# All tokens loaded channels first in the head of a fused hybrid block, two blocks un-normed in u's product

## The chip, the cores and the metric

The kernel runs on one NeuronCore of one Trainium2 chip. A core has a matrix engine (TensorE, PE in the profile), VectorE (DVE), ScalarE (ACT), GpSimd (POOL) and SyncE (SP, which here only issues DMAs), each with its own instruction queue, and 16 DMA engines that all queues share. The metric is the device time of one execution in microseconds. The kernel before takes 1488.93 us (median of three runs, 1485.58 to 1492.47).

## The reference

One layer of a hybrid block on 1040 tokens (16 learned meta tokens, then 1024), D = 1024, everything in float32:

```python
def _mixer(xn, w_in, ...):
    q, k, v, f_logit, u, gates = split(xn @ w_in)
    y_a = forgetting_attention(q, k, v, f_logit, b_forget) @ w_attn_out
    z = gelu(s5(u, ...))                       # 32 groups of 16 channels, 64 complex states each
    zg = z @ w_glu
    y_s = zg[:, :D] * sigmoid(zg[:, D:])
    g = sigmoid(gates)
    return (g[:, :D] * y_a + g[:, D:] * y_s) @ w_o

h = concatenate([meta, x])
h = h + mixer(rmsnorm(h, norm_mix_g))          # rmsnorm(x) = x * rsqrt(mean(x*x) + eps) * g
h = h + conv_ffn(rmsnorm(h, norm_ffn_g))
return rmsnorm(h, norm_final_g)[16:]
```

Only the first lines matter here: the norm of all tokens, u = xn @ w_u (512 columns), and what runs beside and behind it, which is the S5 recurrence on u and the gates' product.

## The kernel before, in words

Matrices are multiplied channels first: a product needs its input as "features", 128 channels on the partitions (8 chunks k) and tokens along the row. For float32 accuracy each operand is split into a high part (rounded to TensorE's fast format) and a low part, and each product takes three matmuls: high by high, low by high, high by low. `xhi` and `xlo` hold the normed features of all 1040 tokens and stay for the whole mixer. The low part on VectorE is called a cut here.

The head computes u in four token blocks, `UBLK` = 272, 256, 256 and 256 tokens, each in four column groups m. One block is 4 x 8 x 3 = 96 matmuls (`part`, L327 to L329). Rows of x come in nine `TILES` (16 meta tokens, then eight of 128).

- Block 0 is loaded channels first (`x0t` into `xa`). Its features are x times gamma only (L350 and L353); the norm's factor per token is applied to the finished product when VectorE copies it from PSUM (L377), from `rsB`, the factor spread to all partitions by three small transposes (L370) and a copy (L372).
- The other tiles are loaded with tokens on the partitions (`xt`). For each, ScalarE squares and sums (L174), VectorE and GpSimd make the factor (L176, L178), VectorE multiplies the tile by factor and gamma (L340), TensorE transposes it in eight pieces (L191), ScalarE makes the high parts (L193) and VectorE the low ones (L129). Tiles 0 to 2, which are block 0, go through the same at the end of u, since the later products need normed features.
- u is copied into `usb` (L387) and stored to `u_d` by 32 DMAs (L394); SyncE issues those of m = 0 and 2, GpSimd those of m = 1 and 3.
- The gates' product is called dense (L159 to L161), 72 matmuls a chunk of 128 columns. A chunk's weights are loaded by GpSimd (`raw`, L140), cast to the high part (L146), negated into `wlo` (L135) and completed there by an accumulating DMA of the same weights (L136). The weights of chunk 8, `g0`, have buffers of their own and an early load (L398).
- The S5 part (`ssm`) first makes tables of its discretised coefficients on VectorE (L1453 to L1459 and others). The scheduler may not start them ahead of the features of tiles 3 and 4 (`ready`). Then come four quarters q of the channels: load U from `u_d`, products, a scan on VectorE (L1748), output products (L1770, L1772), a store to `y_d`. The steps of the four quarters are woven into the dense chunks.
- Behind the dense chunks stand the forget gate (L518) and the GLU on z (L219), for which 32 SyncE DMAs load z from `y_d` (L543).

Which instruction comes when on each engine is not written out: a scheduler in the framework orders each engine's queue from the dependences, the buffers (a tag with so many of them) and its own estimates. Buffers are shared by tag: `Wi`, `Gm`, `sy`, `Tm`, `tq` belong to the S5 part and serve the head before it.

Of the kernel before, what the change touches and what calls it, by code (L numbers as in the profile page):

```python
# [50 lines left out]
def block_kernel(ctx, tc, x, meta, g1, x0t, g1t, w_q, w_k, w_v, w_f, w_u, w_g, b_f, w_ao, lam_d, bw_d, cw_d,  # L51
# [76 lines left out]
    def split_lo(eng, out_, src, hi):  # L128
        return eng.tensor_tensor(out_, src, hi.bitcast(F), ALU.subtract)  # L129
# [40 lines left out]
    def norm_factor(pl, src, n, bufs=10, sq=None):  # L170
# [3 lines left out]
        S.activation(sq[:n], src, AF.Square, accum_out=ss[:n])  # L174
        va = pl.tile([P, 1], F, tag="vr", name="vr", bufs=3)
        V.tensor_scalar(va[:n], ss[:n], 1.0 / D, EPS, ALU.mult, ALU.add)  # L176
        rs = pl.tile([P, 1], F, tag="rs", name="rs", bufs=bufs)
        GP.tensor_tensor(rs[:n], va[:n], nhalf[:n], ALU.pow)  # L178
        return rs
# [107 lines left out]
    xa = [sp.tile([P, 4, UN], F, tag="tq", name="xa", bufs=3) for _ in range(2)]  # L287
    g1T = n1.tile([P, KD], F, name="g1T")
    S.dma_start(g1T, g1t)
    S.dma_start(xm, meta)  # L290
# [15 lines left out]

    place = dict(zip((3, 4, 1, 2, 5, 6), xts))
    place[0] = xm

    def load_x(i):  # L310
        load(place[i], x[P * (i - 1):P * i])

    for i in range(1, 7):
        load_x(i)
# [19 lines left out]
    def factors(i):  # L334
        n = TILES[i][1]
        return norm_factor(n1, place[i][:n], n)

    def features(i, rs, behind=None):
        t, n = TILES[i]
        xn = V.scalar_tensor_tensor(out=place[i][:n], in0=place[i][:n], scalar=rs[:n], in1=g1B[:n],  # L340
                                    op0=ALU.mult, op1=ALU.mult)
        if behind is not None:
            after(xn, behind)
        return to_feature(place[i], n, xhi, xlo, t)[-1]

    first = [mm_ps() for _ in range(4)]
    for j in range(4):
        for k in (2 * j, 2 * j + 1):
            src, hi = xa[j // 2][:, k % 4], xhi[:, k, :UN]
            cp_ = S.activation(hi, src, AF.Copy, scale=g1T[:, k:k + 1])  # L350
            if k == 1:
                after(g1_load, cp_)
            V.scalar_tensor_tensor(out=xlo[:, k, :UN], in0=src, scalar=g1T[:, k:k + 1], in1=hi.bitcast(F),  # L353
                                   op0=ALU.mult, op1=ALU.subtract)
        S.copy(uh[j], uraw[j])
        split_lo(V, ul[j], uraw[j], uh[j])
        for m in range(4):
            for k in (2 * j, 2 * j + 1):
                part(first[m], m, k, 0, UN)
    for i in (7, 8):  # L360
        place[i] = sp.tile([P, D], F, tag="Tm", name="xt", bufs=2)
        load_x(i)

    rs0 = [factors(i) for i in range(3)]
    tp = t_ps()
    for i, rs in enumerate(rs0):
        t, n = TILES[i]
        rb = sp.tile([P, P], F, tag="wi", name="rb", bufs=2)
        V.tensor_copy(rb[:n], rs[:n].broadcast_to([n, P]))
        PE.transpose(tp[:, t:t + n], rb[:n], ident[:n, :n])  # L370
    rsB = sp.tile([P, UN], F, tag="wr", name="rsB", bufs=2)
    S.copy(rsB, tp[:, :UN])  # L372
    for i in (3, 4):
        ready = features(i, factors(i))
    n_log = len(ssm_log)
    for m in range(4):
        V.tensor_tensor(us[m][:, :, :UN // CH], by_chunks(first[m][:, :UN]), by_chunks(rsB), ALU.mult)  # L377

    for b, (t, n) in enumerate(UBLK[1:]):
        if b:  # L380
            for i in (3 + 2 * b, 4 + 2 * b):
                last = features(i, factors(i))
# [1062 lines left out]
def ssm(tc, after, sp, s_ps, ident, u_d, y_d, lam_d, bw_d, cw_d, d_sk, l_dt):  # L1445
# [27 lines left out]
    S.dma_start(ldt, l_dt.partition_broadcast(P))  # L1473

    lam = sm([P, 2, G])
    S.dma_start(lam, lam_d)
# [308 lines left out]
def _laid_out(x, meta_tokens, norm_mix_g, w_in, b_forget, w_attn_out, ssm_lambda_re, ssm_lambda_im, ssm_b_re, ssm_b_im,  # L1785
# [17 lines left out]
    x0 = _np.concatenate([meta_tokens, x[0]])[:UN]  # L1803
# [3 lines left out]
    return dict(x=x[0], meta=meta_tokens, g1=norm_mix_g[0], x0t=by_rows(x0.T), g1t=norm_mix_g[0].reshape(KD, P).T, w_q=blocks(q), w_k=blocks(k), w_v=by_rows(v),  # L1807
# [29 lines left out]
```

## Time and profile before

| | us |
|---|---|
| median of three runs | 1488.93 |
| lowest and highest run | 1485.58 and 1492.47 |
| span of the profiled execution | 1485.7 |
| TensorE busy in it | 1440.4 |
| VectorE, ScalarE, GpSimd busy | 1071.4, 712.2, 742.1 |
| first matmul | 7.32 |
| first dense matmul | 73.53 |
| first GLU matmul in an unbroken run | 239.17 |

Rows of the trace give the start, the duration, the engine, the source line, the operation with output and input tiles, the shape, and in brackets how long the engine stood idle just before and what released it. A row with "x4" joins four like instructions. Starts of matmuls, not their durations, show the pace, since they overlap in the pipeline.

### The profile page before, as it was taken

Reading aid. Unit: us, or ns where it says so; the run is one execution under the profiler, and the core shown is the slowest. Engines: PE = TensorE matmul, PEld = TensorE weight load, DVE = VectorE, ACT = ScalarE, POOL = GpSimd, SP = SyncE. Lnnn points to the kernel's source line nnn. Section 1 sums busy time; section 2 is a strip of 40 time slices with the busy share of each in tenths; the row PEclk is TensorE's granted clock in tenths of the full one; section 3 lists DMA queues with packets and bytes.
Section 4 is the critical chain, followed back from the end, with each engine's and each line's share of the span. In section 5 each row is a group of like instructions: output and inputs, shape, how many; then the busy total and the mean of one; then the engine's idle time right before and its main releaser. Section 6 shows DMA issues by size and latency. Waiting matters only on the chain. (4 is left out here: it accounts for less than half of the span.)

```text
span 1485.7 us, 26584 instructions
## 1 busy us (share of the span) xinstructions
PE 1440.4 (97%) x9712; PEld 1358.8 (91%) x9712; DVE 1071.4 (72%) x2173; ACT 712.2 (48%) x1384; POOL 742.1 (50%) x850
## 2 busy tenths in 40 slices
PE   7999997999999999999999999999999999998997
PEld 7989996998899999999888999999999999777886
DVE  6879648881566676647468987888877776788785
ACT  6434675541555665543546534444444445543433
POOL 1311125752456465524863144455544426789766
PEclk9999999999999999999999999999999999999999
DMA  6366571551127342047885135676653215765513
GB/s 246 86 157 157 128 163 50 177 160 43 48 79 178 93 111 90 26 148 256 257 158 185 57 109 141 178 199 188 174 143 100 84 57 180 286 203 148 168 40 114
DMA packets 91032, 206.72 MB, mean 139 GB/s; under 512 B 14651, under 2 KB 25531, under 8 KB 90517
## 3 DMA queue, kind: packets, MB, share of 16 engines
q1 hardware_dynamic: 69380, 159.73, 32.9%
q0 software_dynamic: 15296, 34.63, 13.2%
q10 hardware_dynamic: 6224, 10.65, 1.9%
q8 instruction: 77, 1.26, 0.3%
q14 instruction: 55, 0.44, 0.1%
HBM read 165.90 MB, written 69.35 MB: 158 GB/s over the span
## 5 line engine op out<-in xcount | busy, mean ns | idle before, releaser
L159 PE MATMUL mm<-xhi,whi 128*128 128x342 f32 (+2 forms) x488 | 159.4, 327 | 1.0 <-DVE q L129 1.0
L161 PE MATMUL mm<-xhi,wlo 128*128 128x342 f32 (+2 forms) x488 | 158.3, 325 | 0.0
L160 PE MATMUL mm<-xlo,whi 128*128 128x342 f32 (+2 forms) x488 | 157.7, 324 | 0.0
L1079 POOL TENSOR_TENSOR ov<-ov,og 128x1024 f32<-128x1024 f32 x21 | 51.1, 2434 | 125.6 <-ACT og L1078 121.7
L129 DVE TENSOR_TENSOR sw<-sf,sw 128x512 fp32r<-128x512 f32 x72 | 66.6, 925 | 50.0 <-ACT sw L1070 49.8
L1070 ACT CAST sw<-sf 128x512 fp32r<-128x512 f32 x72 | 44.9, 624 | 106.2 <-POOL sf L1196 74.5
L159 PEld LDWEIGHTS mm<-xhi,whi 128*128 128x128 f32 x488 | 91.9, 188 | 2.1 <-PE sp L714 0.8
L161 PEld LDWEIGHTS mm<-xhi,wlo 128*128 128x128 f32 x488 | 91.8, 188 | 0.3
L160 PEld LDWEIGHTS mm<-xlo,whi 128*128 128x128 f32 x488 | 91.9, 188 | 0.2
L763 ACT CAST th<-tp 128x256 fp32r<-128x256 f32 (+3 forms) x120 | 56.2, 472 | 62.5 <-PE tp L756 30.1
L129 DVE TENSOR_TENSOR tl<-tp,th 128x256 fp32r<-128x256 f32 (+3 forms) x120 | 65.2, 547 | 25.1 <-ACT th L763 23.7
L1196 POOL TENSOR_TENSOR sf<-raw,sf 128x512 f32<-128x512 f32 x36 | 59.1, 1641 | 44.8 <-DVE sw L129 44.7
L1196 POOL TENSOR_TENSOR sf<-raw 128x512 f32<-128x512 f32 x36 | 48.0, 1332 | 66.9 <-DMA raw<-in_w_up_dram 35.9
L221 PE MATMUL mm<-xhi,sw 128*128 128x258 f32 (+1 forms) x288 | 81.0, 281 | 0.0
L219 PE MATMUL mm<-xhi,sw 128*128 128x258 f32 (+1 forms) x288 | 80.8, 281 | 0.0
L220 PE MATMUL mm<-xlo,sw 128*128 128x258 f32 (+1 forms) x288 | 80.7, 280 | 0.0
L728 POOL TENSOR_SCALAR pt<-pt,nm 128x144 f32<-128x144 f32 (+4 forms) x72 | 51.8, 731 | 48.5 <-DVE nm L727 47.5
L1248 DVE SCALAR_TENSOR_TENSOR ov<-hv,cwt,ov 128x1024 f32<-128x1024 f32 x36 | 72.5, 2014 | 0.1
L1070 ACT CAST sw<-raw 128x512 fp32r<-128x512 f32 x70 | 43.0, 621 | 53.3 <-PE sp L221 25.5
L726 ACT ACTIVATE pt<-pt,nm 128x144 f32<-128x144 f32 (+4 forms) x72 | 52.9, 735 | 26.1 <-DVE nm L725 25.7
L719 DVE CUSTOM_DVE_ANT_0 pt<-sp,fb 128x328 f32<-128x328 f32 (+8 forms) x112 | 46.4, 430 | 20.0 <-PE sp L714 11.1
L756 PE MATMUL tp<-ident,pt 128*128 128x128 f32 (+1 forms) x360 | 58.3, 270 | 0.1
(708 smaller groups left out, 5702.1 us busy)
## 6 DMA issues: line engine op xcount, KB each, us to landing
raw<-in_w_up_dram SPq DMA_DIRECT2D x44, 512.0 KB, 3.6
t_d<-in_w_dn_dram POOLq DMA_DIRECT2D x44, 256.0 KB, 7.0
ar<-a_d SPq DMA_DIRECT2D x44, 256.0 KB, 5.1
wr<-t_d SPq DMA_DIRECT2D x44, 256.0 KB, 2.8
a_d<-ov SPq DMA_DIRECT2D x21, 512.0 KB, 2.6
wr<-in_w_dn_dram SPq DMA_DIRECT2D x33, 256.0 KB, 3.8
t_d<-in_w_dn_dram SPq DMA_DIRECT2D x22, 256.0 KB, 4.2
t_d<-t_d SPq DMA_DIRECT2D x22, 256.0 KB, 4.7
```

The lines of the kernel that those rows point to most:

```text
L129: return eng.tensor_tensor(out_, src, hi.bitcast(F), ALU.subtract)
L159: yield PE.matmul(ps, whi[:, i, :], ahi[:, i], start=(i == 0), stop=False)
L160: yield PE.matmul(ps, whi[:, i, :], alo[:, i], start=False, stop=False)
L161: yield PE.matmul(ps, wlo[:, i, :], ahi[:, i], start=False, stop=(i == k - 1))
L219: PE.matmul(ps, a[0][:, i], bh, start=(i == 0 and not joins), stop=False, skip_group_check=True)
L220: PE.matmul(ps, a[0][:, i], bl, start=False, stop=False, skip_group_check=True)
L221: PE.matmul(ps, a[1][:, i], bh, start=False, stop=(i == kh - 1), skip_group_check=True)
L756: PE.transpose(tp[:kn, o:o + n], p_[:n, k0:k0 + kn], ident[:n, :n])
L763: S.copy(th[:kn, z:tw], tp[:kn, z:tw])
L1070: S.copy(hi, src)
L1196: sums.append(GP.tensor_tensor(f_, a, b, op))
L1248: V.scalar_tensor_tensor(out=o, in0=h_[:, j:SEQ + j], scalar=cwc(j, m), in1=o, op0=ALU.mult, op1=ALU.add)
```

## The change

- All tokens are also loaded channels first: block 0 from `x0t` as before, blocks 1 to 3 from a new input `xbt` (3.1 MB in all). The rows of x are still loaded, for the squares. The load of gamma spread over all partitions goes.
- Blocks 0 and 1 go un-normed into u's product. The product is copied to `usb` by ScalarE, and after all of u VectorE multiplies the first 528 columns of each `usb` by the factors in place.
- Blocks 2 and 3 are multiplied by the factors channels first (`normed_features`) before their products. Blocks 0 and 1 go through the same behind the products of block 2, and `ready` is now the last of these.
- x is no longer transposed; each tile's factor is spread and transposed (nine small transposes).
- The first loads are cut into one k, one k, and then two each; the loads follow in the order block 1, rows 5 to 8, block 2, block 3, rows 1 to 4.
- Block 1 lies in the buffers `Wi`, block 2 in `Tm`, block 3 in `Gm`.
- Three small loads move from ScalarE's queue to GpSimd's.

```diff
-    S.dma_start(xm, meta)
+    GP.dma_start(xm, meta)
...
-    for j in range(4):
-        load(xa[j // 2][:, 2 * (j % 2):2 * (j % 2) + 2], x0t[:, 2 * j:2 * j + 2])
-        load(uraw[j], w_u[:, 2 * j:2 * j + 2])
-    xts = [sp.tile([P, D], F, tag=tag, name="xt", bufs=n) for tag, n in (("Wi", 2), ("Gm", 2), ("sy", 3)) for _ in range(n)]
-    g1B = xts.pop(4)
-    g1_load = S.dma_start(g1B, g1.partition_broadcast(P))
...
+    FIRST = [(0, 1), (1, 1), (2, 2), (4, 2), (6, 2)]
+    for k, n in FIRST:
+        load(xT[0][k // 4][:, k % 4:k % 4 + n], x0t[:, k:k + n])
+        load(uraw[k // 2][:, k % 2:k % 2 + n], w_u[:, k:k + n])
+
+    def load_block(b, tag):
+        xT[b] = [sp.tile([P, 4, UBLK[b][1]], F, tag=tag, name="xT", bufs=2) for _ in range(2)]
+        for h_ in range(2):
+            load(xT[b][h_], xbt[b - 1, :, 4 * h_:4 * h_ + 4])
...
+    load_block(1, "Wi")
+    for i in range(5, 9):
         load_x(i)
...
+    def factors(b):
+        tp = t_ps()
+        t0, n_ = UBLK[b]
+        for i in TB[b]:
+            t, n = TILES[i]
+            rs = norm_factor(n1, place[i][:n], n, behind=head[0])
+            rb = rbs[:n, i % 3]
+            V.tensor_copy(rb, rs[:n].broadcast_to([n, P]))
+            PE.transpose(tp[:, t - t0:t - t0 + n], rb, ident[:n, :n])
+        S.copy(spread[b], tp[:, :n_])
+
+    def features(b, k):
+        t, n = UBLK[b]
+        src, hi = xT[b][k // 4][:, k % 4], xhi[:, k, t:t + n]
+        cp_ = S.activation(hi, src, AF.Copy, scale=g1T[:, k:k + 1])
+        cut = V.scalar_tensor_tensor(out=xlo[:, k, t:t + n], in0=src, scalar=g1T[:, k:k + 1], in1=hi.bitcast(F),
+                                     op0=ALU.mult, op1=ALU.subtract)
+        return cp_, cut
+
+    def normed_features(b):
+        t, n = UBLK[b]
+        for q in range(2):
+            V.tensor_tensor(xT[b][q], xT[b][q], spread[b].unsqueeze(1).broadcast_to([P, 4, n]), ALU.mult)
+        return [features(b, k)[1] for k in range(KD)][-1]
...
+    load_block(2, "Tm")
+    load_block(3, "Gm")
+    for i in range(1, 5):
         load_x(i)
...
     for m in range(4):
-        V.tensor_tensor(us[m][:, :, :UN // CH], by_chunks(first[m][:, :UN]), by_chunks(rsB), ALU.mult)
...
+        S.copy(us_part(0, m), by_chunks(first[m][:, :UN]))
+    for k in range(KD):
+        features(1, k)
+    for b in (2, 3):
+        factors(b)
+    for m in range(4):
+        ps = u_product(1, m)
+        S.copy(us_part(1, m), by_chunks(ps[:, :UBLK[1][1]]))
+    for b in (2, 3):
+        last = normed_features(b)
+        if b == 3:
+            for q in (0, 1):
+                factors(q)
+            n_log = len(ssm_log)
+            for q in (0, 1):
+                ready = normed_features(q)
         for m in range(4):
-            ps = mm_ps()
-            for k in range(KD):
-                part(ps, m, k, t, n)
-            S.copy(us[m][:, :, t // CH:(t + n) // CH], by_chunks(ps[:, :n]))
-        if b == 2:
-            for i in range(3):
-                features(i, rs0[i], last)
+            ps = u_product(b, m)
+            S.copy(us_part(b, m), by_chunks(ps[:, :UBLK[b][1]]))
+    for m in range(4):
+        ub = us[m][:, :, :rs01.shape[1] // CH]
+        V.tensor_tensor(ub, ub, by_chunks(rs01), ALU.mult)
...
-    S.dma_start(ldt, l_dt.partition_broadcast(P))
+    GP.dma_start(ldt, l_dt.partition_broadcast(P))
...
-    S.dma_start(lam, lam_d)
+    GP.dma_start(lam, lam_d)
```

More of the change, by code (lines that the diff above doesn't have):

```diff
@@ L168, in run, with norm_factor @@
             pass
-    def norm_factor(pl, src, n, bufs=10, sq=None):
+    def norm_factor(pl, src, n, bufs=10, sq=None, behind=None):
         if sq is None:
@@ L173, in norm_factor @@
         ss = pl.tile([P, 1], F, tag="ss", name="ss", bufs=3)
-        S.activation(sq[:n], src, AF.Square, accum_out=ss[:n])
+        sa = S.activation(sq[:n], src, AF.Square, accum_out=ss[:n])
+        if behind is not None:
+            after(sa, behind)
         va = pl.tile([P, 1], F, tag="vr", name="vr", bufs=3)
@@ L332, in by_chunks @@
         return a.rearrange("p (n j) -> p j n", j=CH)
[L334 to L344, printed above, removed]
-    first = [mm_ps() for _ in range(4)]
@@ L347, in block_kernel @@
[L347 to L356, printed above, removed]
+    head = []
@@ new lines, in block_kernel @@
+    TB = [(0, 1, 2), (3, 4), (5, 6), (7, 8)]
+    spread = {}
+    rbs = sp.tile([P, 3, P], F, tag="dt8", name="rb", bufs=1)
+    rs01 = sp.tile([P, UN + UBLK[1][1]], F, tag="wr", name="rsB", bufs=2)
+    spread[0], spread[1] = rs01[:, :UN], rs01[:, UN:]
+    for b in (2, 3):
+        spread[b] = sp.tile([P, UBLK[b][1]], F, tag="wi", name="rsB", bufs=2)
+    def factors(b):
[8 more added lines that the diff above has]
+        S.copy(spread[b], tp[:, :n_])
@@ new lines, in u_product, with us_part @@
+    def u_product(b, m):
+        ps = mm_ps()
+        for k in range(KD):
+            part(ps, m, k, *UBLK[b])
+        return ps
+    def us_part(b, m):
+        t, n = UBLK[b]
+        return us[m][:, :, t // CH:(t + n) // CH]
+    first = [mm_ps() for _ in range(4)]
+    for k0, n in FIRST:
+        j, sl = k0 // 2, slice(k0 % 2, k0 % 2 + n)
+        for k in range(k0, k0 + n):
+            features(0, k)
+        cp_ = S.copy(uh[j][:, sl], uraw[j][:, sl])
+        split_lo(V, ul[j][:, sl], uraw[j][:, sl], uh[j][:, sl])
@@ L357, in block_kernel @@
         for m in range(4):
-            for k in (2 * j, 2 * j + 1):
+            for k in range(k0, k0 + n):
                 part(first[m], m, k, 0, UN)
-    for i in (7, 8):
-        place[i] = sp.tile([P, D], F, tag="Tm", name="xt", bufs=2)
+    head.append(cp_)
+    load_block(2, "Tm")
+    load_block(3, "Gm")
+    for i in range(1, 5):
         load_x(i)
[L364 to L370, printed above, removed]
```

26 lines of the change are left out of this document (10 added, 16 removed).

## The prediction

> **What bounds the kernel now.** I read the page first, then the windows of the head, then the order in time on TensorE. The page says which engine sets the length.
>
> ```profile
> span 1485.7 us, 26584 instructions
> ...
> PE 1440.4 (97%) x9712; PEld 1358.8 (91%) x9712; DVE 1071.4 (72%) x2173; ACT 712.2 (48%) x1384; POOL 742.1 (50%) x850
> ```
>
> TensorE is idle for only 45 us in all (1485.7 - 1440.4). The windows (start and end, then busy time of each engine, granted clock, DMA share, GB/s) show where some of that idle time lies.
>
> ```profile
> 20.00:40.00 20.00, 16.87 (x119) 16.41 (x119) 18.31 (x57) 9.66 (x20) 3.96 (x6) 0.83 0.31 124
> ...
> 80.00:100.00 20.00, 17.28 (x110) 16.63 (x109) 12.43 (x31) 7.04 (x16) 1.74 (x5) 0.91 0.78 184
> 100.00:120.00 20.00, 20.00 (x137) 19.75 (x135) 19.75 (x33) 8.70 (x18) 1.58 (x3) 1.00 0.54 112
> ```
>
> Two stretches matter: the head up to 100 us, which the change rewrites, and the one before the GLU, shown further down. From 100 us on TensorE is busy throughout. TensorE in time:
>
> ```profile
> 7.32 0.60 PE L327 MATMUL mm<-xhi,uh 128*128 128x272 f32 x1 [7.32 <-ACT uh L355]
> ...
> 22.05 0.60 PE L191 MATMUL sp<-ident,xt 128*128 128x128 f32 x4
> 22.48 0.60 PE L191 MATMUL tp<-ident,xt 128*128 128x128 f32 x4
> ...
> 26.21 1.12 PE L191 MATMUL sp<-ident,xt 128*128 128x128 f32 x4 [3.13 <-DVE vr L176]
> 31.59 0.41 PE L329 MATMUL mm<-xhi,ul 128*128 128x256 f32 x1
> 31.80 0.41 PE L327 MATMUL mm<-xhi,uh 128*128 128x256 f32 x1
> ...
> 68.53 0.28 PE L328 MATMUL po<-xlo,uh 128*128 128x256 f32 x1
> 68.65 0.28 PE L329 MATMUL po<-xhi,ul 128*128 128x256 f32 x1
> ...
> 72.22 0.63 PE L191 MATMUL sp<-ident,xt 128*128 128x128 f32 x4 [1.68 <-DVE xlo L129]
> 73.53 0.58 PE L159 MATMUL mm<-xhi,g 128*128 128x342 f32 x2 [0.24 <-ACT xhi L193]
> ...
> 74.73 0.32 PE L159 MATMUL mm<-xhi,g 128*128 128x342 f32 x1
> 74.89 0.32 PE L160 MATMUL mm<-xlo,g 128*128 128x342 f32 x1
> ...
> 92.83 0.71 PE L1730 MATMUL sp<-U,Wi 128*128 128x130 f32 x4 [2.72 <-ACT Wi L1714]
> ```
>
> The first column is the start, the last bracket the idle time and who ended it. Block 0 of u ends shortly before the transposes at 22.05, at 21.8; u ends at 68.8, and the gate product ("dense" below) starts at 73.53. After the 3.13 us pause, u's matmuls start 0.21 apart (31.59 to 31.80), 0.12 apart once the clock is back (68.53 to 68.65); the slow rows end at 32.2, so six microseconds run at half pace and 3.0 are lost, as the granted clock of 0.83 for 20 to 40 us says (17% of 20 is 3.4). A dense matmul takes one slot of 0.157 (74.73 to 74.89), a 256-column u matmul one of 0.12.
>
> The second stretch is the end of the SSM:
>
> ```profile
> 194.78 0.39 PE L1770 MATMUL tp<-St,Gm 128*128 128x130 f32 x2
> 224.42 0.33 PE L161 MATMUL mm<-xhi,wlo 128*128 128x384 f32 x1
> 227.62 0.49 PE L518 MATMUL mm<-xhi,wf 128*64 128x272 f32 x1 [2.87 <-POOL wf L129]
> 239.17 0.36 PE L219 MATMUL mm<-zhi,ops 128*128 128x260 f32 x1 [0.93 <-DVE kl L129]
> ```
>
> ```profile
> SPq L543 <- DMA y_d<-Y: 5.1, 1, 5.1
> ```
>
> ```profile
> 188.99 27.62 SPq L543 DMA_DIRECT2D zt<-y_d  x32
> ```
>
> ```profile
> 150.83 0.70 DVE L1456 TENSOR_TENSOR ta<-wr,pc 128x520 f32<-128x520 f32 x1 [3.69 <-ACT wr L1733]
> ...
> 178.86 0.70 DVE L1456 TENSOR_TENSOR ta<-wr,pc 128x520 f32<-128x520 f32 x1 [9.90 <-ACT wr L1733]
> ```
>
> The last SSM output matmuls end at 195.2. SyncE's 32 loads of z wait 5.1 us for the store of that output, run until 216.6, and VectorE's work on z fills the time until the GLU starts at 239.17. So the GLU has two predecessors: the dense products (224.4, then the forget gate) and the last SSM output with z behind it. Everything after it is bound by TensorE, and the order of instructions there is the same in both kernels. What the change is worth is the shift of the GLU's start.
>
> **What the change saves.** (1) The first loads are cut to one k each. The DMA issues of the first 130 us (times issued, size, median us to landing):
>
> ```profile
> raw<-in_w_g_dram POOLq DMA_DIRECT2D x6, 512.0 KB, 5.3
> uraw<-in_w_u_dram SPq DMA_DIRECT2D x4, 512.0 KB, 6.5
> ...
> u_d<-usb POOLq DMA_DIRECT2D x16, 65.0 KB, 7.7
> ```
>
> A 512 KB piece of u's weights needs 6.5. Half of it, and half of its cast behind it, can bring TensorE's first matmul forward by 0 (if the transfer waits for latency alone) up to 2.1; I take 1.6, a start at 5.7, nearer to the end at which the bytes count. (2) The 3.13 pause and its 3.0 of half pace go, since block 1 waits for no factor: 6.1. (3) The transposes: 16 groups of four, 0.43 apart (22.05 to 22.48), are 6.9, and 0.6 for the meta tile; nine transposes of factors return at 0.1, 0.9. Net 6.6. (4) The 1.68 and 0.24 before 73.53: 1.9. From 5.7, block 0 takes the same 14.5, then three blocks of 96 matmuls at 0.12, 34.5, so u ends at 54.7 where dense now begins at 73.53. The sum is 16.2, and the start differs by 18.8, the remainder being short waits between blocks. Gross gain: 19.
>
> For that, blocks 2 and 3 must have features in time. The groups of the head, by line (busy, mean ns):
>
> ```profile
> L340 DVE SCALAR_TENSOR_TENSOR xt<-xt,rs 128x1024 f32<-128x1024 f32 x8 | 10.1, 1276 | 0.7 <-POOL rs L178 0.7
> ...
> L129 DVE TENSOR_TENSOR xlo<-tp,xhi 128x512 fp32r<-128x512 f32 x8 | 5.6, 695 | 0.0
> L353 DVE SCALAR_TENSOR_TENSOR xlo<-xa,g1T,xhi 128x272 fp32r<-128x272 f32 x8 | 3.6, 498 | 4.6 <-ACT xhi L350 4.6
> L377 DVE TENSOR_TENSOR usb<-mm,rsB 128x272 f32<-128x272 f32 x3 | 1.7, 634 | 1.0 <-ACT rsB L372 1.0
> L1456 DVE TENSOR_TENSOR Vm<-sm,sm 128x1024 f32<-128x1024 f32 x1 | 1.2, 1218 | 0.0
> ```
>
> A normed block costs VectorE two multiplies of 128x1024 at 1.22 and eight cuts at 0.50: 6.4, against TensorE's 11.5. That is hidden; without cover it would cost 6.4 a block. VectorE in all loses nine L340 (11.4), sixteen cuts of 128x512 (11.1) and four L377 (2.5), and gets eight multiplies (9.8), 32 more cuts (16) and four multiplies of u by the factor over 528 columns (0.63 x 528/272 = 1.2 each, 4.9): 25 out, 31 in. The extra six are hidden unless the SSM is the bound. The second featurising of blocks 0 and 1 is two L374 pairs (4.9), 16 cuts (8) and the four u multiplies, 17.8 at most, 15.9 where cuts overlap. It starts once the factor rows exist (TensorE's order puts their transposes behind block 2: 5.7 + 14.5 + 2 x 11.5 = 43.2, so 43.5) and ends at 59.4.
>
> **What it gives back.** Three things sit behind it. First the gate weights. GpSimd's queue now:
>
> ```profile
> 64.99 4.05 POOL L394 DMA_DIRECT2D u_d<-usb  x7
> ...
> 83.41 0.53 POOL L394 DMA_DIRECT2D u_d<-usb  x1 [2.10 <-DMA wlo<-in_w_g_dram]
> ```
>
> ```profile
> DMA to landing us min/median/max: 6.4/7.6/11.5
> ```
>
> The second fence is for the low halves of the gate weights, which an accumulating DMA makes. The last row shows a store that waits for a weight transfer issued before it to land: the queue holds only so many, some eight, at a time. In the changed order the first dense chunk is chunk 9, not the preloaded chunk 8, and its accumulate stands behind eight u stores, which wait for the second u multiply (43.5 + four multiplies, four cuts and two u multiplies, 4.9 + 2.0 + 2.4 = 52.8), and two raw loads. The loads and the accumulate each wait for one of the first three stores to land, 7.7 after issue: 60.5. Landing 66.9 to 72.0, 68.1 at the median. TensorE stands from 54.8, two matmuls in, to 68.1: 13.3, plus about 3 at half pace as after the 3.13 pause. The lower bound is the accumulate issued as soon as its ScalarE source is ready, 56.5, and landed at 62.9: 8.1.
>
> The Trainium skill, "DMA: Bandwidth & Descriptors", section "Anatomy of one DMA", fits a GpSimd DMA as 2.0 us plus bytes over 436 GB/s, an estimate of 3.2 us for these 512 KB; the trace's 6.4 to 11.5 doesn't agree. By the page the landing would be 63.7 and the stall 8.9, within the bounds above.
>
> Chunk 8's load is late as well. Its buffer (tag Wi) now holds block 1's x until the second featurising has read it (59.4), and on GpSimd it is behind eight more u stores, of which the last waits for the first accumulate (68.1). Issue 68.6, landed about 74, two ScalarE casts to 76. Its accumulate stands behind GpSimd work on the SSM tables, the last of which waits for VectorE at about 75.5. So: issue 76.2, landing 82.6 to 83.8. TensorE, 28 matmuls later (7 us at half pace, 75.3), stands again until 83: 7.7, and 2 at half pace. Bounds: 0 (it lands by 75) and 12 (the 11.5 landing).
>
> The sum for the dense products: -18.8 + 13.3 + 3 + 7.7 + 2, less the 2.72 at 92.83 and the 1.8 that its clock of 0.91 in 20 us costs (the SSM is no longer awaited there), +2.7. The end of dense goes from 224.4 to about 227, with 220 and 232 as the ends.
>
> The second is the start of the SSM's tables, which wait for `ready`. VectorE:
>
> ```profile
> 31.04 0.18 DVE L1453 TENSOR_SCALAR sm<-sm 128x32 f32<-128x32 f32 x1
> ...
> 106.13 0.68 DVE L1456 TENSOR_TENSOR ta<-wr,pc 128x520 f32<-128x520 f32 x1
> ```
>
> They run from 31.04 in the gaps of the norm and reach the first scan step at 106.13. They will begin at 59.4, unbroken. VectorE's busy time (third pair) between these two points is this:
>
> ```profile
> 31.04:106.13 75.09, 69.93 (x523) 67.40 (x523) 59.90 (x202) 25.91 (x51) 19.85 (x46) 0.97 0.47 115
> ```
>
> Of the 59.9, 18.9 is norm work of seven tiles (1.28 and two cuts, 2.7 each), which leaves 41.0 for the tables and 15.2 of waits. The first scan step comes at 100.4 if no wait remains and 115.6 if all do; I take 106, since TensorE's table products come when dense lets them, so no change.
>
> The third is the order on TensorE. Before, 185 dense matmuls follow the last SSM output; in the changed order 133 do, so 52 more, 8.2 us, stand ahead of it. With dense ending 2.7 later, the last output comes 10.9 late; with dense at its low end (220), 3.8. SyncE's loads and z follow. Against it: fraw is now loaded ahead of z, so the forget gate's 2.87 wait goes and what VectorE does for it comes out of z's way. Less these, the GLU starts 1 to 8 later; I take 3.5, nearer the low end, because both stalls were costed at median landings and the chain of waits can shorten each, but not the order of the 52. Without those reasons the ends are -5 and +11.
>
> The moved small loads (meta, l_dt, lam) go to GpSimd, which has little to do at the start; their readers, block 0's factors and the tables, come after block 1. Zero.
>
> **Rivals.** (A) As above, given back: 1485.7 + 3.5 = 1489.2 on the profiled span. The span is the lowest run's time (1485.58), 3.2 under the median of the three runs, so 1492.5 against 1488.93. (B) Faster: the weights land at the lower bounds. The first stall is 5.2 shorter, the second and its half pace (9.7) go; dense ends at 212, and the last output 4.2 earlier than now in spite of the 52. With the 2.87 gone too the GLU starts 7 earlier, 6 to 12 as the tables follow: 1476 to 1483. For it: raw loads land in 5.3. Against: no wlo landed under 6.4, and there are two such stalls in a row. (C) Slower: the SSM chain on VectorE becomes the bound. Its slack is what it waited for TensorE, 9.90 at 178.86 and 3.69 earlier, 13.6 in all; it decides once the first scan step is later than 106.1 + 13.6 = 119.7. If the tables need their whole 75 us from 59.4, that step comes at 134.5 and the GLU 15 later: 1504; halfway, 1497. For it: the windows from 100 us show VectorE at 19.75 of 20; against: the 115.6 above. (D) The change doesn't speed the first products: the loads are bound by transfer, 3.1 MB more stand in the queue, block 1 starts as late as now. Then the gross gain is 14 rather than 19, but the stalls shorten with it, since the weights land when they land: 1493 to 1496.
>
> **How the numbers follow.** A has 0.48, B 0.18, C 0.24, D 0.10. A difference of 0.5%, 7.4 us, is about what a measurement of this kernel can tell from no change: 1481.5 and 1496.4 are the borders. A spreads from 1480 to 1499 and gives 0.02 to faster, 0.39 to same, 0.07 to slower; B 0.12 faster and 0.06 same; C 0.03 same and 0.21 slower; D 0.05 same and 0.05 slower. Together 0.14 faster, 0.53 same, 0.33 slower. The range takes all of A and the nearer parts of B and C: 1480 to 1505.
>
> **What would show it.** Right: TensorE's first matmul before 6.5, no L191-like transposes of x, u ended near 55, then a TensorE wait of 8 to 14 us released by an accumulate into the gate weights, another at 75 to 83; VectorE's tables beginning near 59; the last SSM output near 200, the GLU near 242.7. Dense matmuls some 0.31 apart instead of 0.157 behind each wait would show the half pace. The Trainium skill, "TensorE: Matmul & The Clock Gate", section "HAM oscillation", says that TensorE pauses above about 3.4 us bring the slow clock back; here 3.13 sufficed. By the page both stalls would be followed by one such stretch, which is what the sum has. Wrong: dense running from 55 without a wait (then B and beyond), the first scan step after 119 (C), or u ending after 60 (D).

## The result, and the profile after

The changed kernel takes 1498.79 us (median of five runs, 1496.74 to 1500.8) against 1488.93 for the kernel before (five runs by now, with the same median and range, 1485.58 to 1492.47). The ratio is 1.0067 with a 95% interval from 1.0048 to 1.0086: slower by 0.7%. The profiled execution's span is 1494.8 us against 1485.7.

The page of the changed kernel: TensorE is busy 4.4 us less than before and idle 13.5 us more (1494.8 - 1436.0 = 58.8 against 45.3), VectorE has 9.6 us more.

```profile
span 1494.8 us, 26525 instructions
...
PE 1436.0 (96%) x9646; PEld 1353.3 (91%) x9646; DVE 1081.0 (72%) x2201; ACT 720.6 (48%) x1413; POOL 742.2 (50%) x853
```

Its windows (start and end, length, then busy time of PE, PEld, DVE, ACT, POOL, granted clock, DMA share, GB/s):

```profile
20.00:40.00 20.00, 20.00 (x169) 19.84 (x168) 12.95 (x33) 17.98 (x42) 7.32 (x11) 1.00 0.72 256
40.00:60.00 20.00, 18.02 (x148) 17.33 (x146) 16.26 (x29) 14.65 (x33) 5.60 (x11) 1.00 0.43 116
60.00:80.00 20.00, 6.35 (x26) 6.06 (x27) 19.44 (x117) 1.71 (x2) 10.72 (x32) 0.57 1.04 243
80.00:100.00 20.00, 14.33 (x81) 13.45 (x80) 18.54 (x53) 3.75 (x6) 0.87 (x1) 0.83 0.33 61
```

TensorE now runs through 20 to 40, where it had 16.87 of 20 before, and stands for most of 60 to 80, where it had 18.09. VectorE is the other way round: 12.95 busy in 20 to 40 (18.31 before), and 19.44 and 18.54 from 60 to 100.

TensorE in order of time shows the steps; line numbers are those of the changed kernel.

```profile
5.38 0.59 PE L334 MATMUL mm<-xhi,uh 128*128 128x272 f32 x1 [5.38 <-ACT uh L392]
...
56.89 0.28 PE L336 MATMUL po<-xhi,ul 128*128 128x256 f32 x1
58.53 0.42 PE L159 MATMUL po<-xhi,whi 128*128 128x342 f32 x1 [1.36 <-ACT usb L422]
...
72.77 0.65 PE L161 MATMUL po<-xhi,wlo 128*128 128x342 f32 x1 [13.09 <-DMA wlo<-in_w_g_dram]
...
86.23 0.65 PE L161 MATMUL mm<-xhi,g 128*128 128x342 f32 x1 [5.67 <-DMA g<-in_w_g_dram]
86.69 0.49 PE L159 MATMUL mm<-xhi,g 128*128 128x342 f32 x1
...
208.35 0.39 PE L1805 MATMUL tp<-St,Gm 128*128 128x130 f32 x2
...
230.39 0.29 PE L553 MATMUL mm<-xhi,wf 128*64 128x272 f32 x1
...
241.49 0.56 PE L221 MATMUL mm<-zhi,ops 128*128 128x260 f32 x1 [3.40 <-DVE kl L129]
...
257.91 0.46 PE L221 MATMUL mm<-zhi,ops 128*128 128x260 f32 x1 [2.30 <-ACT ms L234]
```

u ends at 57.0 instead of 68.8. The two waits for gate weights (13.09 and 5.67) give that away, and the dense products end at 230.4 instead of 224.6. The last SSM output (208.35) is 13.6 later than the 194.78 of before.

VectorE's table work and the first scan step of each quarter in the changed kernel, then, in the kernel before, two of the tables and the step that was not shown yet:

```profile
61.88 0.65 DVE L1488 TENSOR_SCALAR sm<-sm 128x32 f32<-128x32 f32 x3
...
109.44 0.70 DVE L1491 TENSOR_TENSOR ta<-wr,pc 128x520 f32<-128x520 f32 x1 [4.44 <-ACT wr L1768]
...
112.62 1.22 DVE L1491 TENSOR_TENSOR Vm<-sm,sm 128x1024 f32<-128x1024 f32 x1
...
119.92 1.34 DVE L1491 TENSOR_TENSOR tm<-sm,sm 128x1152 f32<-128x1152 f32 x1
...
130.59 0.70 DVE L1491 TENSOR_TENSOR ta<-wr,pc 128x520 f32<-128x520 f32 x1 [0.72 <-ACT wr L1768]
...
164.82 0.70 DVE L1491 TENSOR_TENSOR ta<-wr,pc 128x520 f32<-128x520 f32 x1 [8.46 <-ACT wr L1768]
...
192.80 0.70 DVE L1491 TENSOR_TENSOR ta<-wr,pc 128x520 f32<-128x520 f32 x1 [9.84 <-ACT wr L1768]
```

```profile
100.68 1.22 DVE L1456 TENSOR_TENSOR Vm<-sm,sm 128x1024 f32<-128x1024 f32 x1
...
104.86 1.34 DVE L1456 TENSOR_TENSOR tm<-sm,sm 128x1152 f32<-128x1152 f32 x1
...
119.52 0.70 DVE L1456 TENSOR_TENSOR ta<-wr,pc 128x520 f32<-128x520 f32 x1
```

The first step is 3.3 later than before (106.13), the second 11.1, the third and fourth 14.0 and 13.9. So most of the delay does not come from the start of the first scan: 7.8 of the 13.9 appear between the first step and the second, which are 21.2 apart instead of 13.4, because `Vm` of the second quarter (112.62) and `tm` of the third (119.92) are made in that stretch; before, both stood ahead of the first step (100.68 and 104.86). Another 2.9 comes up to the third step, and nothing is caught up after it. The end of the chain, on VectorE in both kernels (before, then after):

```profile
237.21 0.68 DVE L129 TENSOR_TENSOR z2l<-zf,z2h 128x520 fp32r<-128x520 f32 x1
...
240.27 0.70 DVE L129 TENSOR_TENSOR zlo<-zf,zhi 128x520 fp32r<-128x520 f32 x1
```

```profile
248.03 0.69 DVE L129 TENSOR_TENSOR z2l<-zf,z2h 128x520 fp32r<-128x520 f32 x1
...
250.55 0.68 DVE L129 TENSOR_TENSOR zlo<-zf,zhi 128x520 fp32r<-128x520 f32 x1
```

The last cuts of z are 10.8 and 10.3 later. The GLU starts 2.3 later (241.49 against 239.17) and then waits and slows (257.91 above); the first attention product comes 7.5 later (before, then after), and the rest of the span adds 1.6.

```profile
381.27 0.17 PE L714 MATMUL sp<-kl,qz 128*32 128x16 f32 x1
```

```profile
388.74 0.17 PE L749 MATMUL sp<-kl,qz 128*32 128x16 f32 x1
```

### The profile page after: what moved, and what is told of

It reads as the page before. It is cut to its first block, busy times and chain, and to the rows that moved or that the text cites. A ratio compares the mean times of both kernels' runs of the same rounds, so it can differ in the third digit from the quotient of the medians.

```text
span 1494.8 us, 26525 instructions
## 1 busy us (share of the span) xinstructions
PE 1436.0 (96%) x9646; PEld 1353.3 (91%) x9646; DVE 1081.0 (72%) x2201; ACT 720.6 (48%) x1413; POOL 742.2 (50%) x853
## 3 DMA queue, kind: packets, MB, share of 16 engines
q0 software_dynamic: 15392, 34.74, 13.5%
## 5 line engine op out<-in xcount | busy, mean ns | idle before, releaser
L129 DVE TENSOR_TENSOR sw<-raw,sw 128x512 fp32r<-128x512 f32 x70 | 55.7, 799 | 5.7 <-ACT sw L1105 5.2
```

## The experiments

Two theories stood against each other. *Weights*: the head's loss sits in the two weight waits. *VectorE*: the tables begin too late, and the scans carry that to z. A third, *order*, was the prediction's own: the last output is late because 52 more dense matmuls stand ahead of it. Each ratio is to the kernel before on the same chip; that kernel's own median was between 1487.65 and 1489.35 there, so differences between medians of different groups are good to two or three microseconds. The scheduler orders each variant anew, so an edit can also move instructions that it doesn't name.

**swap.** Chunk 8's buffer is no longer held by block 1.

```diff
-        tag, bufs = ("Gm", 2) if i in (5, 6) else ("sy", 3)
+        tag, bufs = ("Wi", 2) if i in (5, 6) else ("sy", 3)
-    load_block(1, "Wi")
+    load_block(1, "Gm")
-    load_block(3, "Gm")
+    load_block(3, "Wi")
```

> The kernel after, with one thing changed: block 1 lies in the buffers Gm and block 3 and rows 5 and 6 in Wi, so that chunk 8's gate weights need not wait until block 1 has been featurised a second time. Theory W (the late gate weights give the gain back): both TensorE waits for weights (13.1 and 5.7 us, about 6 more at half pace) shrink to under 4 in all, the last SSM output comes at 192 or before and the time falls by 10 to 18 us, to 1481 to 1489. Rival S (the SSM, whose tables start only when the second featurising is done, sets the end): the two waits go, but the last SSM output still ends at 200 to 206, TensorE stands instead before the GLU, and the time stays within 4 us of 1498.8.

1491.34 us, ratio 1.0024 (1.0009 to 1.0039): 7.5 less than the changed kernel. In swap, first GpSimd's DMAs for chunk 8, then two groups of TensorE's waits (us in total, times, longest):

```profile
37.59 0.59 POOL L433 DMA_DIRECT2D g<-in_w_g_dram  x1
...
45.83 0.93 POOL L136 DMA_DIRECT2D g<-in_w_g_dram  x1 [3.43 <-ACT rsB L360]
```

```profile
PE mm L159 <- ACT gs L478: 5.2, 2, 5.0
...
PE po L161 <- DMA wlo<-in_w_g_dram: 1.0, 1, 1.0
```

The accumulate for chunk 8 goes out at 45.83 instead of 80.69, ahead of the stores of u, so the dense products start with chunk 8 as u ends (55.78), and end at 220.4, ten earlier. The last output moves only from 209.0 to 205.7. The buffer is the cause of the weight waits, and they were part of the loss; the gain lies between what the two theories expected. The wait of 5.0 is not one for weights: ScalarE's sigmoid of the gates (`gs`) waits 5.1 there for the store of an earlier result to land. A wait of this kind is left in swap_early (6.6), both_order (7.5), earlier (6.4) and earlier_ch (7.0) too, and no run removes it.

**early.** The tables may begin behind block 3's features instead of behind the second featurising.

```diff
-    after(ssm_log[n_log], ready)
+    after(ssm_log[n_log], last)
```

> The kernel after, with one thing changed: the SSM's tables may start after block 3's features, not after the second featurising of blocks 0 and 1. Theory W: the waits for gate weights stay (about 13 and 5 us), so TensorE is as late as now and the time stays within 4 us of 1498.8. Rival S: the tables start at 43 to 50, the last SSM output comes 6 to 12 us earlier although TensorE still waits for weights, and the time falls to 1486 to 1493.

1490.12 us, ratio 1.0020 (1.0006 to 1.0033): 8.7 less. VectorE's first table work of the kind shown at 61.88 begins at 40.5, and the scan steps come at 101.3, 118.9, 150.9 and 179.9, which are those of the kernel before within 5 us. The last output ends at 196.4. TensorE still waits 17.0 us for chunk 8's weights, and dense ends at 225.9. So the late tables cost about as much as the weight waits, and each edit alone leaves the other chain late. With the tables ready sooner the scheduler also puts only 533 dense matmuls ahead of the last output, where the changed kernel has 587; the run called order, below, tries that without the early tables.

**swap_early.** Both edits.

> Both changes together: block 1 in Gm with block 3 in Wi, and the tables free to start after block 3's features. If W alone holds, as fast as the exchange of buffers alone (1481 to 1489). If S alone holds, as fast as the early tables alone (1486 to 1493). If each gates the other, faster than either by 4 us or more: 1472 to 1482.

1486.19 us, ratio 1.0000 (0.9984 to 1.0016): 12.6 less than the changed kernel, and level with the one before. Dense ends at 213.4, eleven ahead of before, but the last output at 201.0 is still 5.6 behind it. The gain over each edit alone, 5.2 and 3.9, falls short of the 1472 to 1482 that was expected if each gated the other. From here on VectorE's chain is the later one.

**first_only.** The kernel before with only the first loads and casts of the head cut to one k each.

```diff
-    for j in range(4):
-        load(xa[j // 2][:, 2 * (j % 2):2 * (j % 2) + 2], x0t[:, 2 * j:2 * j + 2])
-        load(uraw[j], w_u[:, 2 * j:2 * j + 2])
+    FIRST = [(0, 1), (1, 1), (2, 2), (4, 2), (6, 2)]
+    for k, n in FIRST:
+        load(xa[k // 4][:, k % 4:k % 4 + n], x0t[:, k:k + n])
+        load(uraw[k // 2][:, k % 2:k % 2 + n], w_u[:, k:k + n])
```

> The kernel before, with only its first loads cut into one k, one k and then two each, as in the kernel after. If the earlier first matmul is worth what the prediction gave it, TensorE starts at 5.4 to 5.9 and the time falls by up to 1.6 us, which three rounds can hardly tell from 1488.9; if the bytes bound block 0, TensorE waits between the pieces instead, block 0 ends at 21.5 to 22 as before, and the time is 1488.9.

1487.74 us, ratio 1.0001 (0.9985 to 1.0017). TensorE starts at 5.69 instead of 7.32, but the last matmul of block 0 begins at 21.3, against an end at 21.8: the later pieces set the end, and the early start is spent on half pace and on waits for them. It is worth nothing here. In this kernel the transposes behind block 0 wait for VectorE in any case (26.70, against 26.21 before), so for the changed kernel the end of block 0 says more than the time.

**st_act.** The changed kernel with the stores of u on ScalarE's queue instead of GpSimd's.

```diff
-            (GP if m % 2 else SY).dma_start(um[g], us[m][GC * g:GC * g + GC])
+            (S if m % 2 else SY).dma_start(um[g], us[m][GC * g:GC * g + GC])
```

> The kernel after, with one thing changed: the sixteen u stores of m = 1 and 3 are issued by ScalarE instead of GpSimd, so no store stands ahead of the weights' accumulates. The order of matmuls on TensorE stays as it is but for a few. If the GpSimd queue makes the weights late (the prediction's first stall), the first accumulate is issued at 57 to 59 instead of 61.6 and lands by 66, and the first TensorE wait falls from 13.1 to 5 to 9 us, the second stays or falls; the time falls by 3 to 8 us. If the weights wait for something else, both waits stay and the time stays at 1498.8.

1500.43 us, ratio 1.0086 (1.0061 to 1.0110). It says little of the queue: the scheduler now put chunk 8 first, whose buffer block 1 still holds, and TensorE waited 13.6 for its ScalarE cast and 11.0 for its accumulate. Inconclusive.

**order.** The changed kernel with the dense matmuls held behind the SSM outputs, as before: the first matmul of chunk 13 waits for the last output of quarter 1, those of chunks 14 and 15 for that of quarter 2 (quarters counted from 0).

```diff
+    BEHIND = {(5, 0): 1, (6, 0): 2, (7, 0): 2}
...
+            if q_ is not None and not tanh:
+                first_ = next(steps)
+                after(first_, y_last[q_])
+                yield first_
```

> The kernel after, with only an order added on TensorE: the first matmul of chunk 13 may not stand ahead of the SSM's output product of quarter 1, those of chunks 14 and 15 not ahead of quarter 2's. 524 instead of 587 dense matmuls then stand ahead of the last SSM output. Theory O (the dense matmuls ahead of the last output make z late, the third part of the prediction): the last output ends near 200 instead of 209, z and the GLU follow, and the time falls by 5 to 9 us, to 1490 to 1494, with TensorE's waits for weights as they are. Rival P (TensorE's own lateness sets the GLU's start): dense and the forget gate end at 238 as now, and the time moves by less than 3 us.

1501.60 us, ratio 1.0093 (1.0063 to 1.0123), not faster than the changed kernel. The dense matmuls of one of the three lines between the last SSM output and the end of dense, in the changed kernel and in order (the count in brackets):

```profile
208.98:230.38 21.40, 14.22 (x45) 1.00 0.70 144
```

```profile
205.27:236.20 30.93, 20.80 (x66) 1.00 0.67 144
```

133 matmuls of the three lines follow the last output in the changed kernel, as predicted, and 196 in order: 63 more, worth 9.9 at 0.157. The last output came only 3.7 earlier (205.3), and TensorE got new waits for tables (2.8 and 1.1), so dense ended 5.8 later. The scan steps are where they were (109.2, 130.3, 164.6) up to the last (188.4 instead of 192.8). So at most 3.7 of the 13.6 can be put down to the 52 matmuls: for the rest they had filled time in which the SSM's products lacked VectorE's tables, as the new waits show.

**both_order.** swap_early with such an order.

> The exchange of buffers and the early tables together, and an order added on TensorE: chunk 13 not ahead of quarter 1's output product, the last two thirds of chunk 14 and all of chunk 15 not ahead of quarter 2's. 544 instead of 642 dense matmuls then stand ahead of the last SSM output. Theory O: the last output ends at 182 to 188 instead of 201, TensorE's dense products end at 213 to 217, and the GLU runs without its waits for z: 1470 to 1479, faster than both kernels. Rival: the SSM on VectorE can't go faster, its scans wait for VectorE itself instead of ScalarE's copies, the last output stays at 196 or later and the time at 1483 to 1488.

1493.81 us, ratio 1.0035 (1.0020 to 1.0050): 7.6 slower than swap_early by the medians, with TensorE at 17.25 of 20 us from 140 to 160 and 15.22 from 160 to 180, where swap_early has 20.00 in both. Two of its new waits are for VectorE's tables (1.8 and 3.0). The last output comes 1.2 earlier (199.8) and dense 14 later.

**mul_pool and mul_norm.** swap_early, with the four multiplies of u by the factor moved from VectorE to GpSimd (mul_pool), and with the multiplies of x in blocks 0 and 1 moved too (mul_norm).

```diff
-        V.tensor_tensor(ub, ub, by_chunks(rs01), ALU.mult)
+        GP.tensor_tensor(ub, ub, by_chunks(rs01), ALU.mult)
...
-            V.tensor_tensor(xT[b][q], xT[b][q], spread[b]...
+            (GP if b < 2 else V).tensor_tensor(xT[b][q], xT[b][q], spread[b]...
```

> The exchange of buffers and the early tables together, and the four multiplies of u by the factors (4.7 us of VectorE) done by GpSimd. Theory V (VectorE's work ahead of and among the tables sets the last SSM output, and with it z and the GLU): the scan of quarter 1 starts 3 to 5 us earlier than 121.3, the last output ends at 196 to 198 instead of 201, the time falls by 2 to 5 us to 1481 to 1484. Rival O (TensorE's queue sets it, as 656 instead of 642 dense matmuls now stand ahead of the last output): the scans of quarters 2 and 3 wait longer for ScalarE's copies, the last output stays at 200 or later and the time at 1485 or above.

> As the run before it, and the four multiplies of blocks 0 and 1 by the factors (4.8 us of VectorE) go to GpSimd too. 546 dense matmuls stand ahead of the last SSM output. Theory V: the scan of quarter 1 starts 7 to 10 us earlier than 121.3, the last output ends at 188 to 194, the time falls by 6 to 12 us to 1474 to 1480. Rival (GpSimd is too slow for it: blocks 0 and 1 get their second features 5 us or more later, and TensorE and the u stores wait): the last output stays at 198 or later, or dense ends after 225, and the time stays at 1484 or above.

mul_pool 1490.51 us, ratio 1.0016 (0.9998 to 1.0034), no gain; mul_norm 1502.48 us, ratio 1.0098 (1.0081 to 1.0115), 16 more than swap_early. VectorE and then GpSimd in mul_norm:

```profile
46.38 0.39 DVE L1494 SCALAR_TENSOR_TENSOR sm<-sm,sm 128x32 f32<-128x32 f32 x3
46.69 16.68 DVE L1488 TENSOR_SCALAR sm<-sm 128x32 f32<-128x32 f32 x1
63.29 0.18 DVE L1491 TENSOR_TENSOR sm<-sm 128x32 f32<-128x32 f32 x1
63.39 0.17 DVE L1488 TENSOR_SCALAR sm<-sm 128x32 f32<-128x32 f32 x1
```

```profile
47.00 5.35 POOL L374 TENSOR_TENSOR xa<-xa,rsB 128x1088 f32<-128x1088 f32 x2
51.99 5.05 POOL L374 TENSOR_TENSOR xT<-xT,rsB 128x1024 f32<-128x1024 f32 x2
56.71 6.61 POOL L425 TENSOR_TENSOR usb<-usb,rsB 128x528 f32<-128x528 f32 x4
```

One VectorE instruction on 32 columns, which takes 0.17 elsewhere, lasts 16.68 us and ends with the last of GpSimd's eight multiplies (47.00 to 63.32). Work handed to GpSimd was not taken off VectorE here; it stopped VectorE for longer than it takes there (9.5 in swap_early). In mul_pool, beside GpSimd's 9.6 us for the four multiplies of u, VectorE instructions of this kind lasted 3.43 (two of them) and 1.75. In mul_norm TensorE then waited 12.9 for the normed low parts of the first blocks.

**earlier.** swap, with the tables allowed from the end of block 1's un-normed low parts on, where VectorE had 7 of 20 us free.

```diff
-        features(1, k)
+        start = features(1, k)[1]
...
-    after(ssm_log[n_log], ready)
+    after(ssm_log[n_log], start)
```

> The exchange of buffers, and the SSM's tables free to start behind the last cut of block 1 (near 30 us) instead of block 3's (near 43) or the second featurising (62); nothing moves to another engine. VectorE was idle for 7 of the 20 us from 20 to 40 us. Theory V (VectorE's table and scan work, counted from where it may start, sets the last SSM output): the scan of quarter 1 starts 6 to 10 us before 121.3, the last output ends at 188 to 194, dense ends at 210 to 216, and the time falls to 1474 to 1482, below both kernels. Rival: table work ahead of the features of blocks 2 and 3 delays u (ends after 60 instead of 56.7) and u's store by as much as it gains, and the time stays at 1484 to 1490.

1483.01 us, ratio 0.9960 (0.9946 to 0.9973): faster than both kernels. The window of 20 to 40, and the scan steps, in earlier:

```profile
20.00:40.00 20.00, 20.00 (x168) 19.84 (x167) 17.43 (x85) 17.37 (x41) 5.80 (x8) 1.00 0.73 258
```

```profile
96.01 0.70 DVE L1491 TENSOR_TENSOR ta<-wr,pc 128x520 f32<-128x520 f32 x1 [1.90 <-ACT wr L1768]
...
114.41 0.70 DVE L1491 TENSOR_TENSOR ta<-wr,pc 128x520 f32<-128x520 f32 x1 [0.43 <-ACT wr L1768]
...
148.64 0.70 DVE L1491 TENSOR_TENSOR ta<-wr,pc 128x520 f32<-128x520 f32 x1 [6.25 <-ACT wr L1768]
...
176.63 0.70 DVE L1491 TENSOR_TENSOR ta<-wr,pc 128x520 f32<-128x520 f32 x1 [9.85 <-ACT wr L1768]
```

VectorE is busy 17.43 there instead of 12.95, TensorE still 20.00; the first scan step is 13.4 ahead of the changed kernel's and the others 16.2. The last output ends at 192.8, dense at 214.2.

**leave_out.** swap_early without the factors of blocks 0 and 1: the four multiplies of u and the four of x ahead of the second features are left out, so u and the later products of these two blocks use un-normed tokens. The second features themselves are still made, with all their cuts.

```diff
-        V.tensor_tensor(ub, ub, by_chunks(rs01), ALU.mult)
+        pass
...
-        for q in range(2):
+        for q in range(2 if b > 1 else 0):
```

> The exchange of buffers and the early tables together, without the four multiplies of u by the factors and the four of blocks 0 and 1 ahead of their second features: u and the later features of these tokens stay un-normed, so nine to ten us of VectorE's work are left out, and no other engine does them. Theory V: the scan of quarter 1 starts 6 to 9 us before 121.3, the last output ends at 190 to 195, and the time falls by 5 to 10 us against 1486.2. If something else sets the last output (TensorE's queue, the loads of U), it stays at 198 or later and the time within 3 us of 1486.2.

1476.99 us, ratio 0.9916 (0.9891 to 0.9941): 9.2 less than swap_early by the medians, 12.5 by the two ratios, for about 9.5 us of VectorE work (in swap_early 4.6 for the four multiplies of u, 4.9 for the four of x). The last output ends at 191.5 instead of 201.0, 9.5 earlier. So hardly any of that work was covered by other waits.

**earlier_ch.** earlier, with the factors laid out in the order of u's chunks, so that VectorE reads them in a row.

```diff
+        if b < 2:
+            S.copy(rsj[:, :, t0 // CH:(t0 + n_) // CH], by_chunks(tp[:, :n_]))
...
-        V.tensor_tensor(ub, ub, by_chunks(rs01), ALU.mult)
+        V.tensor_tensor(ub, ub, rsj, ALU.mult)
```

> As the kernel with the earliest tables (1483.0), and ScalarE writes the factors of blocks 0 and 1 a second time in the order in which u lies in its buffer, so VectorE's four multiplies of u read both operands in a row; the order of matmuls on TensorE is the same. If the strided read is what makes these 1.18 us each, they take 0.65 to 0.75, VectorE is 1.8 to 2.1 us ahead, the last output ends 1 to 2 us earlier than 192.8 and the time falls by 0.5 to 2 us, at the edge of what five rounds tell. If the form of the operands doesn't matter, they stay at 1.18 and so does the time.

1481.97 us, ratio 0.9949 (0.9933 to 0.9966). The intervals of earlier and earlier_ch overlap, so a gain over earlier is not shown. The multiply by itself became shorter, as the groups by line show (busy, mean ns; earlier, then earlier_ch):

```profile
L425 DVE TENSOR_TENSOR usb<-usb,rsB 128x528 f32<-128x528 f32 x4 | 4.7, 1256 | 0.0
```

```profile
L428 DVE TENSOR_TENSOR usb<-usb,rsB 128x528 f32<-128x528 f32 x4 | 2.6, 702 | 0.0
```

## Why the prediction was right or wrong

**The time.** 1492.5 was forecast, with 1480 to 1505 as the range; 1498.79 lies within, 6.3 above the forecast, inside rival C's 1497 to 1504 and at the very end of A's spread (1480 to 1499). Same was the likeliest sign at 0.53 with slower at 0.33; slower it was.

**What the change saves: right in the mechanism, 2.3 short.** TensorE starts at 5.38 (5.7), there is no transpose of x, and u ends at 57.0 (54.7). Most of the shortfall is in the term "block 0 takes the same 14.5": it took 16.3, since its later pieces come when they did before (first_only). So term (1), 1.6 for the smaller first loads, was next to nothing: block 0 ended at 21.7 instead of 21.8.

**The weights: right, with sizes that made up for each other.** The first wait was 13.1 as forecast (13.3), but from later on both sides: it began at 59.7, not 54.8, and ended at 72.8, not 68.1. That the sizes agree is luck. GpSimd's queue in the changed kernel:

```profile
55.49 4.26 POOL L429 DMA_DIRECT2D u_d<-usb  x8 [11.63 <-ACT usb L422]
...
61.61 0.91 POOL L136 DMA_DIRECT2D wlo<-in_w_g_dram  x1 [0.66 <-DMA u_d<-usb]
...
73.01 0.53 POOL L429 DMA_DIRECT2D u_d<-usb  x1 [3.13 <-DMA wlo<-in_w_g_dram]
73.87 0.57 POOL L433 DMA_DIRECT2D g<-in_w_g_dram  x1 [0.33 <-DMA u_d<-usb]
...
80.69 0.87 POOL L136 DMA_DIRECT2D g<-in_w_g_dram  x1 [2.25 <-ACT g L135]
```

The eight stores stand ahead of the accumulate, which went out at 61.6 (60.5 forecast); it took 11.2 to land, close to the 11.5 that was the longest before, where the forecast took the median of 7.6. The store at 73.01 waits 3.13 for it, and chunk 8's load stands behind that store: its accumulate goes at 80.69 (76.2) and the second wait is 5.7 (7.7). Behind each wait some 15 matmuls started 0.285 apart (73.22 and 73.51, for one) instead of 0.157: the half pace of the forecast, at 1.9 and 2.1 us where it had 3 and 2. Dense ended at 230.4, inside the 220 to 232, 3.4 past the forecast. That the buffer `Wi` is the root of it is shown by swap; that the stores on GpSimd's queue are, beside it, st_act could not tell.

**The step that failed: the second of the three things given back, the tables.** "The first scan step comes at 100.4 if no wait remains and 115.6 if all do; I take 106 [...] so no change." The step itself came at 109.4, within the bounds, and the start of the tables at 61.9 was nearly as forecast (59.4). What failed is the reading of it: the first step was taken as the sign that the tables are done. It only needs those of its own quarter. The others were put off behind it, and the delay was 3.3 at the first step, 11.1 at the second and 13.9 at the fourth. For the same reason rival C was given the wrong test: "it decides once the first scan step is later than 106.1 + 13.6 = 119.7", with the slack of 13.6 from VectorE's waits at 150.83 and 178.86. These waits are not slack. In the changed kernel, with VectorE late, they are 8.46 and 9.84, and in earlier, with VectorE early, 6.25 and 9.85: most of them stays whichever way VectorE goes. VectorE waits there for a product of its own table: in the changed kernel it has `Vm` ready at 183.0, TensorE transposes it from 185.27 and multiplies with it from 189.42, ScalarE copies, and the scan step comes at 192.80. Where TensorE had less in between (order), the last wait was 5.7, not zero. What rival C describes, the SSM chain on VectorE as the bound, is what happened beside the weight waits, and "the extra six are hidden unless the SSM is the bound" turned on its own condition: the count of 31 us held (13.2 and 7.2 of cuts, 7.1 and 2.5 of multiplies of x, 4.7 for u are 34.7, of which 3.6 were there before), and leave_out puts 9 to 12 us of time on 9.5 us of it, the multiplies by the factors of blocks 0 and 1.

**The third thing, the order on TensorE: a small part at most.** The count was right (133 behind the last output), the late output too (13.6, beyond the 10.9). But order put 196 matmuls behind the last output and won 3.7 on it and lost time, while early, earlier and leave_out, which change when VectorE gets to the tables or what it has to do, brought the last output to 196.4, 192.8 and 191.5. In earlier and leave_out 133 and 136 dense matmuls follow it, the changed kernel's count or nearly, and it is as early as in the kernel before. There dense ends some 16 us earlier as well, since most of the weight waits are gone too. But swap, which takes away only these, moved the last output by 3.3: the scheduler put 672 dense matmuls ahead of it, and even behind these TensorE waited 1.3 for VectorE's scan (`St`, at 201.65).

**"What the change is worth is the shift of the GLU's start."** The start moved by 2.3 (3.5 forecast), the time by 9.9. The GLU begins on what is there; its later products wait for a low half of z (1.23 at 246.43) and for ScalarE (2.30 at 257.91), whose work for the forget gate comes behind VectorE's last cuts of z. The windows of TensorE alone at two places of the changed kernel's GLU (busy time, granted clock):

```profile
241.00:247.00 6.00, 4.28 (x22) 0.72 0.00 0
...
257.00:262.00 5.00, 4.09 (x21) 0.66 0.35 103
```

Both stops, 3.40 and 2.30, were followed by half pace. Counted from 381.27 and 388.74, the first attention product, the loss was 7.5; that is the point at which the forecast should have been taken.

**The rivals.** B, weights at the lower bounds, did not happen by itself, but swap made most of it: 13.1 and 5.7 of waits for weights became 1.0 (with the 5.0 for ScalarE's sigmoid), dense ended ten earlier, and yet 1491.34 and not 1476 to 1483, because the last output hardly moved. D fell: block 1 began at 21.7, right behind block 0, and the end of u gained 11.8.

## What to carry to other kernels

When work is taken off the busiest engine, look at which engine gets it and whether another chain already fills that engine there: here TensorE lost its transposes, and VectorE's tables, held back by one ordering constraint, made z late. A chain of stages that share an engine is not late or in time by its first step; compare every step, and don't count an idle stretch as slack until it has been seen to shrink. With the constraint moved to where VectorE was free and the preload's buffer kept out of the way (earlier), the same change is faster than both kernels, 0.4%.

## What the hardware showed that was not expected

- **GpSimd holds VectorE off.** mul_norm's rows: 16.68 us for one VectorE instruction that takes 0.17, over a run of eight GpSimd multiplies. The Trainium skill, "SBUF — State Buffer", section "SBUF: two separate sides", tells of a port pair shared by the two engines as an exclusive lock: whoever starts first has it for the whole instruction, and the other blocks; on VectorE's side this is for instructions in a two-port mode, or with two SBUF inputs while GpSimd's reads SBUF. The trace agrees that one blocks, but here VectorE stood over eight GpSimd instructions in a row, not one. The stopped instruction's row names one input (`sm`); whether it ran in such a mode no run shows.
- **The order of a second operand counts.** The same multiply on 128x528 took 1.26 us with the factors read in strides and 0.70 with them in a row (earlier and earlier_ch).
- **A short stop can bring half pace.** A stop of 2.30 us at 257.91, behind two of about 1 us in the twelve before it, was followed by 16 matmuls 0.22 apart instead of 0.12, as after the 3.40 at 241.49. A longer stop of 2.54 at 233.40 in swap was not: the matmuls behind it soon start 0.12 apart (234.03, 234.15, 234.27). So the length of the stop alone does not decide it; what does stays open.
